# RMS norm and a matmul on one core: another opening, and a last pair of tiles in column blocks

## The chip, the cores and the metric

The kernel runs on one core of a Trainium2 chip. A core has a matrix engine (TensorE, PE in the profile, its weight loads PEld), VectorE (DVE), ScalarE (ACT), GpSimd (POOL) and SyncE (SP, which here only issues transfers), a working memory of 128 partitions (SBUF), accumulator banks that PE writes (PSUM), and 16 DMA engines between SBUF and the device's memory. The metric is the device time of one launch in microseconds (us); less is better.

## The reference

```python
batch, seq, dim, out_dim = 16, 1024, 512, 768
rms = np.sqrt(np.mean(x ** 2, axis=-1, keepdims=True) + eps)
x_norm = x / rms * gamma
return np.matmul(x_norm, weight).astype(np.float32)
```

x has 16,384 rows of 512 floats (33.6 MB), weight is 512 x 768 (1.57 MB), the output 16,384 x 768 floats (50.3 MB). Gamma and eps are inputs.

## The kernel before

The rows are worked on in 128 tiles of 128 rows. Two tiles make a pair j (0 to 63), two pairs a group g (0 to 31) of 512 rows. In a group each partition p holds four rows that lie side by side in memory, so a group's load is 128 pieces of 8 KB (1 MB) and its store 128 pieces of 12 KB (1.5 MB). The row scale 1/rms is applied to the output, gamma to the weights, so the matmuls can start before the norms are known.

For each pair:

- POOL casts x to bf16 (`cast`, L68 to L71).
- ACT squares each tile with a running sum (`squares`, L77), then takes the root (L80); DVE forms the reciprocal (L82).
- PE transposes x. It takes two bf16 values as one 32-bit word, so a tile needs two transposes of 128 x 128 words (`transpose_word`, L92), a pair four. They land in one PSUM tile `tp` (two buffers), and DVE copies the pair to SBUF as `xT` (`evac_words`, L98).
- PE multiplies: four blocks of the inner dimension (k) times two column ranges, 512 and 256 wide, so eight matmuls a tile (L121), into an accumulator of two PSUM banks. There are three accumulators, used in turn.
- ACT scales the first tile of the pair to the output buffer (L130), DVE the second (L132). An output buffer holds a group; there are four, used in turn.
- SP stores the group once its fourth tile is scaled (L136). The last group goes out in two halves.

The order is written out by hand, and each engine and each queue works through its own list in that order; waits are put in for every use of a buffer, among them the wait of a scaling for the store that last read its output buffer. While PE multiplies pair j, the four transposes of pair j + 2 are put between its matmuls (L124, L125), one after every second k. Casts run three pairs ahead, norms one. SP issues the load of group g + 6 at the start of group g (L177), and there are eight input buffers.

The opening (L139 to L173): SP issues the first pair of x (as half a group), the two halves of the weights, the other half of group 0, and groups 1 to 5; group 6 follows at the start of the loop. ACT's queue loads gamma. PE turns gamma to a column (L161). Pair 0 is cast, squared and transposed; DVE scales the four row blocks of the weights to bf16 (`w_bf`, L172). Pair 0 runs its matmuls with k outside and its two tiles inside. Then come the squares of pair 1 and the transposes of pairs 1 and 2, and from pair 1 on the loop is as above.

Of the kernel before, what the change touches and what calls it, by code (L numbers as in the profile page):

```python
# [12 lines left out]
F32 = mybir.dt.float32  # L13
BF16 = mybir.dt.bfloat16
AF = mybir.ActivationFunctionType


@with_exitstack
def kernel(
    ctx: ExitStack,  # L20
    tc: tile.TileContext,
    x: bass.AP,
    gamma: bass.AP,
    weight: bass.AP,
    eps: float,
    out: bass.AP,
):
    nc = tc.nc
    P = 128

    x = x.flatten_outer_dims()
    out = out.flatten_outer_dims()
    N, D = x.shape
    _, O = out.shape
    K = D // P
    G = 4
    NG = N // (P * G)
    NP = 2 * NG
    PF = 6
    SPLITS = [(0, 512), (512, O)]  # L40


    xg = x.rearrange("(g p t) d -> g p t d", p=P, t=G)
    og = out.rearrange("(g p t) o -> g p t o", p=P, t=G)

    singles = ctx.enter_context(tc.tile_pool(name="singles", bufs=1))
    xin = ctx.enter_context(tc.tile_pool(name="xin", bufs=PF + 2))
    xbp = ctx.enter_context(tc.tile_pool(name="xb", bufs=4))
    junk = ctx.enter_context(tc.tile_pool(name="junk", bufs=2))
    stats = ctx.enter_context(tc.tile_pool(name="stats", bufs=4))  # L50
    xt_pool = ctx.enter_context(tc.tile_pool(name="xt", bufs=4))
    tpsum = ctx.enter_context(tc.tile_pool(name="tpsum", bufs=2, space=bass.MemoryType.PSUM))
    opsum = ctx.enter_context(tc.tile_pool(name="opsum", bufs=3, space=bass.MemoryType.PSUM))
    outp = ctx.enter_context(tc.tile_pool(name="out", bufs=4))

    x_tiles, xb_tiles, tp_tiles, rstd_tiles, xT_tiles, o_tiles = {}, {}, {}, {}, {}, {}

    def load(g, parts=1):
        xt = xin.tile([P, G, D], F32, name="xt")
        x_tiles[g] = xt  # L60
        n = G // parts
        for i in range(parts):
            nc.sync.dma_start(out=xt[:, i * n:(i + 1) * n, :], in_=xg[g, :, i * n:(i + 1) * n, :])

    def xpair(j):
        return x_tiles[j // 2][:, 2 * (j % 2):2 * (j % 2) + 2, :]

    def cast(j):  # L68
        xb = xbp.tile([P, 2, D], BF16, name="xb")
        xb_tiles[j] = xb  # L70
        nc.gpsimd.tensor_copy(out=xb, in_=xpair(j))  # L71

    def squares(j):
        ssq = stats.tile([P, 2], F32, name="ssq")
        for t in range(2):
            jk = junk.tile([P, D], BF16, name="jk")
            nc.scalar.activation(out=jk, in_=xpair(j)[:, t, :], func=AF.Square,  # L77
                                 accum_out=ssq[:, t:t + 1])
        rms = stats.tile([P, 2], F32, name="rms")
        nc.scalar.activation(out=rms, in_=ssq, func=AF.Sqrt, scale=1.0 / D, bias=eps_sb)  # L80
        rstd = stats.tile([P, 2], F32, name="rstd")
        nc.vector.reciprocal(out=rstd, in_=rms)  # L82
        rstd_tiles[j] = rstd

    def transpose_word(j, t, h):
        if j not in tp_tiles:
            tp_tiles[j] = tpsum.tile([P, 2, 2, P], F32, name="tp")
        words = xb_tiles[j].rearrange("p a d -> p (a d)").bitcast(F32)  # L90
        lo = t * (D // 2) + h * P
        nc.tensor.transpose(out=tp_tiles[j][:, t, h, :], in_=words[:, lo:lo + P], identity=ident_f)  # L92

    def evac_words(j):
        xb_tiles.pop(j)
        tp = tp_tiles.pop(j)
        xT = xt_pool.tile([P, 2, 2, P, 2], BF16, name="xT")
        nc.vector.tensor_copy(out=xT.rearrange("p t h m c -> p (t h m c)"),  # L98
                              in_=tp.rearrange("p t h m -> p (t h m)").bitcast(BF16))
        xT_tiles[j] = xT  # L100

    def transposes(j):
        for t in range(2):
            for h in range(2):
                transpose_word(j, t, h)
        evac_words(j)

    def matmuls(j, tj=None):
        g, h = j // 2, j % 2
        if h == 0:  # L110
            o_tiles[g] = outp.tile([P, G, O], F32, name="ot")
        ot = o_tiles[g]
        xT = xT_tiles.pop(j)
        rstd = rstd_tiles.pop(j)
        acc = [opsum.tile([P, 2, 512], F32, name="ops").rearrange("p a b -> p (a b)") for _ in range(2)]

        order = [(t, k) for k in range(K) for t in range(2)] if j == 0 else \
                [(t, k) for t in range(2) for k in range(K)]
        for n, (t, k) in enumerate(order):
            for i, (lo, hi) in enumerate(SPLITS):  # L120
                nc.tensor.matmul(out=acc[t][:, lo:hi], lhsT=xT[:, t, k // 2, :, k % 2], rhs=w_bf[:, k, lo:hi],  # L121
                                 start=(k == 0), stop=(k == K - 1))

                if tj is not None and i == 0 and n % 2 == 0:  # L124
                    transpose_word(tj, n // 4, n // 2 % 2)  # L125
            if k < K - 1:
                continue
            dst = ot[:, 2 * h + t, :]
            if t == 0:
                nc.scalar.mul(out=dst, in_=acc[t][:, :O], mul=rstd[:, t:t + 1])  # L130
            else:
                nc.vector.tensor_single_scalar(out=dst, in_=acc[t][:, :O], scalar=rstd[:, t:t + 1],  # L132
                                               op=mybir.AluOpType.mult)

    def store(g, lo=0, hi=G):
        nc.sync.dma_start(out=og[g, :, lo:hi, :], in_=o_tiles[g][:, lo:hi, :])  # L136

    with tc.manual_schedule():
        nc.scalar.preload_act_table(AF.Sqrt)  # L139
        g_row = singles.tile([2, P, 2], F32)  # L140
        nc.scalar.dma_start(out=g_row, in_=gamma.rearrange("(h w c) -> h w c", w=P, c=2))
        w_f32 = singles.tile([P, K, O], F32)

        x0 = xin.tile([P, G, D], F32, name="xt")
        x_tiles[0] = x0
        nc.sync.dma_start(out=x0[:, 0:2, :], in_=xg[0, :, 0:2, :])
        for h in range(2):
            nc.sync.dma_start(out=w_f32[:, 2 * h:2 * h + 2, :],
                              in_=weight[2 * h * P:2 * (h + 1) * P, :].rearrange("(w c) o -> w c o", c=2))
        nc.sync.dma_start(out=x0[:, 2:4, :], in_=xg[0, :, 2:4, :])  # L150
        for g in range(1, PF):
            load(g)

        ident_f = singles.tile([P, P], F32)
        make_identity(nc, ident_f)
        eps_sb = singles.tile([P, 1], F32)
        nc.vector.memset(eps_sb, float(eps))  # L157

        gp = tpsum.tile([P, 2, 2], F32, name="tp")
        for c in range(2):  # L160
            nc.tensor.transpose(out=gp[:, c, :], in_=g_row[:, :, c], identity=ident_f[:2, :2])  # L161
        g_sb = singles.tile([P, 2, 2], F32)
        nc.vector.tensor_copy(out=g_sb, in_=gp)  # L163

        cast(0)
        cast(1)
        squares(0)
        transposes(0)

        w_bf = singles.tile([P, K, O], BF16)  # L170
        for k in range(K):
            nc.vector.tensor_single_scalar(out=w_bf[:, k, :], in_=w_f32[:, k, :], scalar=g_sb[:, k % 2, k // 2:k // 2 + 1],  # L172
                                           op=mybir.AluOpType.mult)  # L173

        for j in range(NP):
            if j % 2 == 0 and j // 2 + PF < NG:
                load(j // 2 + PF)  # L177
            if j + 3 < NP:
                cast(j + 3)
            if j == 0:  # L180
                cast(2)
                matmuls(0)
                squares(1)
                transposes(1)
                transposes(2)
            else:
                if j + 1 < NP:
                    squares(j + 1)
                if j + 2 < NP:
                    matmuls(j, j + 2)  # L190
                    evac_words(j + 2)
                else:
                    matmuls(j)
            g = j // 2
            if g == NG - 1:
                store(g, 2 * (j % 2), 2 * (j % 2) + 2)
            elif j % 2:
                store(g)


# [33 lines left out]
```

## Time and profile before

| | |
|---|---|
| median of 5 runs | 215.09 us (214.63 to 215.16) |
| the profiled execution | 214.63 us, span 212.8 us |
| PE busy | 196.4 us (92%) |
| ACT, DVE, POOL busy | 156.1, 110.6, 67.2 us |
| DMA | 85.69 MB, mean 403 GB/s |
| matmuls (L121), 512 and 256 wide | 382 and 274 ns each as recorded |
| transpose (L92) | 275 ns as recorded |
| evacuation (L98), a pair | 680 ns |
| scaling of a tile on ACT (L130), on DVE (L132) | 901, 1018 ns |
| squares of a tile (L77), root (L80) | 619, 295 ns |
| cast of a pair on POOL (L71) | 1041 ns |
| store of a group, issue to landing | median 10.8 us |
| load of a group, issue to landing | median 12.8 us |

The span runs from the first to the last instruction of the profiled execution; the launch adds some 1.8 us around it. Matmuls are pipelined and the recorded length of one holds its way through the array, so a pace is read from the distance of two starts, not from the length. A chain of waits follows the work that ended last back from the end. For a DMA issue, the time to landing is that until its data is in place, with all that stood before it in the queue.

### The profile page before, as it was taken

The page shows a single profiled execution, that of the slowest core. Times are in us where ns is not written, and L with a number is a line of the kernel's source. Part 1 is how long each engine was busy: PE and PEld are TensorE (multiplying, and loading weights), DVE is VectorE, ACT ScalarE, POOL GpSimd, SP SyncE. Part 2 cuts the span into 40 slices and gives each one's busy share as a digit, 9 for nine tenths or more (in the row PEclk, how much of TensorE's full clock was granted, in tenths as well). Part 3 has the DMA queues.
Part 4 walks back from the last instruction along what each step waited for, and adds up shares of the span by engine and source line. Part 5 has one row for each costly group of instructions (what it writes and reads, how often), then busy time and mean ns, then how long its engine had stood idle before and what let it go on. Part 6 is the DMA issues. An engine that isn't in the chain of part 4 may idle for free.

```text
span 212.8 us, 3556 instructions
## 1 busy us (share of the span) xinstructions
PE 196.4 (92%) x1257; PEld 136.9 (64%) x1282; DVE 110.6 (52%) x198; ACT 156.1 (73%) x385; POOL 67.2 (32%) x70
## 2 busy tenths in 40 slices
PE   0579999999999999999999999999999999999980
PEld 0336777767777777777677777767777777777650
DVE  0525446644664466445644565456545654565451
ACT  2356877787778777877787778777877787778840
POOL 1267323332333223322332233323332333230000
PEclk9999999999999999999999999999999999999997
DMA  5999999999999999999999999999999999967777
GB/s 182 423 425 423 428 423 420 420 426 420 436 429 421 423 423 433 422 426 431 423 429 423 433 415 429 432 432 423 420 426 426 423 435 429 404 270 303 303 297 294
DMA packets 9814, 85.69 MB, mean 403 GB/s; under 512 B 1090, under 2 KB 1092, under 8 KB 1860
## 3 DMA queue, kind: packets, MB, share of 16 engines
q1 hardware_dynamic: 9792, 85.46, 95.7%
q8 instruction: 10, 0.16, 0.3%
q14 instruction: 8, 0.07, 0.1%
q10 hardware_dynamic: 4, 0.00, 0.0%
HBM read 35.13 MB, written 50.33 MB: 402 GB/s over the span
## 4 chain that ended last, share of the span: by engine, by line
PE 91%; DMA 2%; DVE 1%; ACT 1%; issue 1%; POOL 0%
PE ops L121 78%; PE tp L92 13%; DMA xt<-in_x_dram 2%; ACT jk L77 1%; POOL xb L71 0%; DVE ot L132 0%; ACT ot L130 0%; DVE xT L98 0%; DVE w_bf L172 0%; ACT rms L80 0%; DVE rstd L82 0%
## 5 line engine op out<-in xcount | busy, mean ns | idle before, releaser
L121 PE MATMUL ops<-w_bf,xT 128*128 128x256 bf16 (+1 forms) x999 | 193.7, 327 | 3.2 <-DVE w_bf L172 1.3
L121 PEld LDWEIGHTS <-xT 128*128 128x128 bf16 x1024 | 100.7, 98 | 59.2 <-issue 2.1
L132 DVE TENSOR_SCALAR ot<-ops,rstd 128x768 f32<-128x768 f32 x64 | 65.1, 1018 | 88.9 <-PE ops L121 88.9
L71 POOL CAST xb<-xt 128x1024 bf16<-128x1024 f32 x64 | 66.5, 1041 | 122.7 <-PE tp L92 111.8
L130 ACT ACTIVATE ot<-ops,rstd 128x768 f32<-128x768 f32 x64 | 57.7, 901 | 44.5 <-PE ops L121 44.5
L77 ACT ACTIVATE jk<-xt 128x512 bf16<-128x512 f32 x128 | 78.8, 619 | 3.3 <-DMA xt<-in_x_dram 3.3
L92 PE MATMUL tp<-ident_f,xb 128*128 128x128 f32 x256 | 68.9, 275 | 5.2 <-POOL xb L71 5.2
L98 DVE COPY xT<-tp 128x1024 bf16<-128x1024 bf16 x64 | 43.4, 680 | 0.4 <-PE tp L92 0.4
L92 PEld LDWEIGHTS tp<-ident_f,xb 128*128 128x128 f32 x256 | 36.0, 142 | 8.4 <-POOL xb L71 5.5
L77 ACT ACTIVATION_READ_ACCUMULATOR jk<-xt 128x1 f32 x128 | 24.3, 190 | 0.0
L80 ACT ACTIVATE rms<-ssq,eps_sb 128x2 f32<-128x2 f32 x64 | 18.9, 295 | 2.1
L82 DVE RECIPROCAL rstd<-rms 128x2 f32<-128x2 f32 x64 | 9.9, 155 | 5.6 <-ACT rms L80 5.6
L161 PE MATMUL tp<-ident_f,g_row 2*128 2x2 f32 x2 | 0.4, 249 | 2.2 <-DMA g_row<-in_gamma_dram 2.2
L172 DVE TENSOR_SCALAR w_bf<-w_f,g_sb 128x768 bf16<-128x768 f32 x4 | 2.2, 614 | 0.0
L139 ACT ACT_TABLE_LOAD x1 | 1.3, 1283 | 0.7 <-PEq L215 0.7
L161 PEld LDWEIGHTS tp<-ident_f,g_row 2*128 2x128 f32 x2 | 0.3, 200 | 2.2 <-POOL ident_f masks.py:199 2.2
L163 DVE COPY g_sb<-tp 128x4 f32<-128x4 f32 x1 | 0.2, 160 | 1.7 <-PE tp L161 1.7
L157 DVE MEMSET eps_sb<- 128x1 f32 x1 | 0.1, 59 | 0.8 <-PEq L215 0.8
masks.py:199 POOL TENSOR_SCALAR_AFFINE_SELECT ident_f<-ident_f 128x128 f32<-128x128 f32 x1 | 0.3, 293 | 0.1
masks.py:197 POOL MEMSET ident_f<- 128x128 f32 x1 | 0.2, 204 | 0.3 <-POOLq L215 0.3
L215 POOL MEMSET const-float32-0.0<- 128x1 f32 x1 | 0.1, 99 | 0.2 <-issue 0.2
L215 POOL MEMSET const-bfloat16-1.0<- 128x1 bf16 x1 | 0.1, 102 | 0.0
(2 smaller groups left out, 0.2 us busy)
## 6 DMA issues: line engine op xcount, KB each, us to landing
out_dram<-ot SPq DMA_DIRECT2D x31, 1536.0 KB, 10.8
xt<-in_x_dram SPq DMA_DIRECT2D x31, 1024.0 KB, 12.8
w_f<-in_weight_dram SPq DMA_DIRECT2D x2, 768.0 KB, 6.8
out_dram<-ot SPq DMA_DIRECT2D x2, 768.0 KB, 4.0
xt<-in_x_dram SPq DMA_DIRECT2D x2, 512.0 KB, 6.5
g_row<-in_gamma_dram ACTq DMA_DIRECT2D x1, 2.0 KB
```

The source lines that it names most:

```text
L71: nc.gpsimd.tensor_copy(out=xb, in_=xpair(j))
L77: nc.scalar.activation(out=jk, in_=xpair(j)[:, t, :], func=AF.Square, accum_out=ssq[:, t:t + 1])
L80: nc.scalar.activation(out=rms, in_=ssq, func=AF.Sqrt, scale=1.0 / D, bias=eps_sb)
L82: nc.vector.reciprocal(out=rstd, in_=rms)
L92: nc.tensor.transpose(out=tp_tiles[j][:, t, h, :], in_=words[:, lo:lo + P], identity=ident_f)
L98: nc.vector.tensor_copy(out=xT.rearrange("p t h m c -> p (t h m c)"), in_=tp.rearrange("p t h m -> p (t h m)").bitcast(BF16))
L121: nc.tensor.matmul(out=acc[t][:, lo:hi], lhsT=xT[:, t, k // 2, :, k % 2], rhs=w_bf[:, k, lo:hi], start=(k == 0), stop=(k == K - 1))
L130: nc.scalar.mul(out=dst, in_=acc[t][:, :O], mul=rstd[:, t:t + 1])
L132: nc.vector.tensor_single_scalar(out=dst, in_=acc[t][:, :O], scalar=rstd[:, t:t + 1], op=mybir.AluOpType.mult)
L139: nc.scalar.preload_act_table(AF.Sqrt)
L161: nc.tensor.transpose(out=gp[:, c, :], in_=g_row[:, :, c], identity=ident_f[:2, :2])
L172: nc.vector.tensor_single_scalar(out=w_bf[:, k, :], in_=w_f32[:, k, :], scalar=g_sb[:, k % 2, k // 2:k // 2 + 1], op=mybir.AluOpType.mult)
```

## The change

The tiles are cut into segments instead of groups: of 1, 2, 1, 2 and 2 tiles, then 29 of four tiles, then 2, 1 and 1. A segment is what one load, one output buffer and one store hold. Each segment's rows lie side by side in memory: a partition's piece of x is 2 KB for a segment of one tile, 4 KB for two, 8 KB for four. There are ten input buffers in place of eight, still four output buffers and three accumulators.

The opening is written anew. SP issues tile 0, tiles 1 and 2, the weights, and then six more segments of x (tile 3 to tile 23). PE runs twelve matmuls on a zeroed tile, whose result nobody reads, in four batches of three: ahead of the turning of gamma, behind it, behind the transposes of tile 0, and behind those of tiles 1 and 2. Tiles 0 to 2 are cast, transposed and evacuated one by one, tiles 0 and 1 cast by DVE. The weights' row blocks are scaled by DVE (0 and 2) and by ACT (1 and 3). Tiles 0, 1 and 2 run their matmuls for k = 0 and 1 first, side by side in three accumulators, then for k = 2 and 3 one by one, each followed by its scaling. Tile 3 follows, with the transposes of pair 2 between its last matmuls.

In the loop, which begins with pair 2, pairs 2 to 5 carry the transposes of the next pair, pair 6 those of pairs 7 and 8, and the later ones those of the pair after next as before. The evacuation is now put into DVE's list right behind the pair's fourth transpose, ahead of the odd tile's scaling. One segment is loaded whenever a pair begins a new segment.

For the last two tiles the matmuls run the 512 columns first for all k, then the 256, into an accumulator of their own each. ACT scales the wide block and stores it on its own queue, DVE scales the narrow one and SP stores it.

```diff
-    PF = 6
+    XBUFS = 10
+    sizes = [1, 2, 1, 2, 2] + [G] * (NT // G - 3) + [2, 1, 1]
+    first = [sum(sizes[:s]) for s in range(NS)]
+    def rows(ap, s):
+        return ap[first[s] * P:(first[s] + sizes[s]) * P, :].rearrange("(p t) d -> p t d", t=sizes[s])
...
+    def evac(j, t=0, n=2):
+        if j not in xT_tiles:
+            xT_tiles[j] = xt_pool.tile([P, 2, 2, P, 2], BF16, name="xT")
+        src = tp_tiles.pop(j).rearrange("p t h m -> p t (h m)").bitcast(BF16)
+        dst = xT_tiles[j].rearrange("p t h m c -> p t (h m c)")
+        nc.vector.tensor_copy(out=dst[:, t:t + n, :], in_=src[:, t:t + n, :])
...
+    def out_tile(i):
+        s = seg_of[i]
+        if s not in o_tiles:
+            o_tiles[s] = outp.tile([P, G, O], F32, name="ot")
+        return o_tiles[s][:, i - first[s], :]
+    def store(i):
+        s = seg_of[i]
+        if i == first[s] + sizes[s] - 1:
+            nc.sync.dma_start(out=rows(out, s), in_=o_tiles[s][:, :sizes[s], :])
...
+        load(0)
+        load(1)
...
+        for s in range(2, XBUFS - 1):
+            load(s)
...
+        def warm_up(n):
+            for _ in range(n):
+                nc.tensor.matmul(out=spare[:, :WIDE], lhsT=warm[:, :P], rhs=warm, start=True, stop=True)
...
+        warm_up(3)
...
+        warm_up(3)
+        ssq = stats.tile([P, 4], F32, name="ssq")
+        cast(0, nc.vector)
+        square(0, ssq[:, 0:1])
+        transpose_tile(0)
+        warm_up(3)
+        cast(1, nc.vector)
+        cast(2, nc.gpsimd)
+        square(1, ssq[:, 1:2])
+        square(2, ssq[:, 2:3])
+        transpose_tile(1)
+        transpose_tile(2)
+        warm_up(3)
+        acc = [accumulator() for _ in range(4)]
+        weights(0, nc.vector)
+        weights(1, nc.scalar)
+        for k in (0, 1):
+            for i in range(3):
+                matmuls(i, acc[i], [k])
+        root(0, 3, ssq)
+        weights(2, nc.vector)
+        weights(3, nc.scalar)
+        cast(3, nc.gpsimd)
+        matmuls(0, acc[0], [2, 3])
+        finish_tile(0, acc[0], nc.scalar)
+        transpose_tile(3)
+        norms(3, 1)
+        matmuls(1, acc[1], [2, 3])
+        finish_tile(1, acc[1], nc.vector)
+        cast(4, nc.gpsimd, 2)
+        matmuls(2, acc[2], [2, 3])
+        finish_tile(2, acc[2], nc.scalar)
+        matmuls(3, acc[3], [0, 1, 2, 3], feeder([2], [0, 0, 2, 2]))
+        finish_tile(3, acc[3], nc.vector)
+        cast(6, nc.gpsimd, 2)
+        cast(8, nc.gpsimd, 2)
+        norms(4, 2)
+        one, two, both = [0, 0, 1, 0, 1, 1, 1, 0], [1, 0, 1, 0, 1, 0, 1, 0], [1, 1, 1, 1, 1, 1, 1, 1]
+        loaded = XBUFS - 1
+        for j in range(2, NP):
+            if seg_of[2 * j] > seg_of[2 * j - 1] and loaded < NS and loaded < seg_of[2 * j] + XBUFS - 1:
+                load(loaded)
+                loaded += 1
...
+            if j < 6:
+                feed = feeder([j + 1], one)
+            elif j == 6:
+                feed = feeder([7, 8], both)
+            elif j + 2 < NP:
+                feed = feeder([j + 2], two)
+            for i, engine in ((2 * j, nc.scalar), (2 * j + 1, nc.vector)):
+                a = accumulator()
+                matmuls(i, a, range(K), feed)
+                finish_tile(i, a, engine)
+        for i in (NT - 2, NT - 1):
+            s = seg_of[i]
+            for lo, hi, engine, queue in ((0, WIDE, nc.scalar, nc.scalar), (WIDE, O, nc.vector, nc.sync)):
+                a = accumulator()
+                for k in range(K):
+                    matmul(i, k, a, lo, hi)
+                dst = out_tile(i)[:, lo:hi]
+                scale(engine, dst, a[:, lo:hi], rstd_of[i])
+                queue.dma_start(out=rows(out, s)[:, 0, lo:hi], in_=dst)
```

`feeder(pairs, gaps)` gives a function that `matmuls` calls between the 512- and the 256-wide matmul of each k; each call issues as many transposes of the listed pairs as the list says, and the evacuation behind a pair's fourth.

## The prediction

> **What bounds the kernel now.** I read the page first (busy shares, slices), then the chain of waits, then the order of time at both ends, then the DMA issues with their times to landing.
>
> ```profile
> PE 196.4 (92%) x1257; PEld 136.9 (64%) x1282; DVE 110.6 (52%) x198; ACT 156.1 (73%) x385; POOL 67.2 (32%) x70
> ...
> PE   0579999999999999999999999999999999999980
> ...
> DMA  5999999999999999999999999999999999967777
> ```
>
> PE is full from slice 3 to the last but one, and the DMA engines are full too until the loads end near 187 us. PE is the bound: ACT's scalings of the even tiles start at 194.29, 197.32 and 200.36, so a pair takes 3.034 us, and without transposes (203.18, 205.78) 2.60 us. A tile's eight matmuls are thus 1.30 us and one transpose is (3.034 - 2.60)/4 = 0.108 us. The work is 128 x 1.30 + 256 x 0.108 = 194.1 us; PE ends at 207.0, so about 13 us are lost before its even pace, which begins with pair 1 at 16.43 (chain of waits, start, length, what):
>
> ```profile
> 0.74 4.57 DMA xt<-in_x_dram
> 5.37 1.04 POOL xb L71
> 6.46 1.13 PE tp L92 x4
> 8.88 4.23 PE ops L121 x14
> 13.14 0.90 ACT ot L130
> 14.04 1.23 ACT jk L77 x4
> 16.43 0.39 PE ops L121
> ```
>
> Pair 0 costs 4.6 us, not 2.6, and then PE waits for an evacuation that stands on DVE behind a reciprocal, behind ACT's squares and scaling. Pair 7, whose transposes and those of pair 8 are the first state that both kernels share, starts at 16.43 + 6 x 3.034 = 34.63. The forecast is when the new kernel reaches that point.
>
> Why pair 0 is slow shows in the weight loads in order of time:
>
> ```profile
> 9.91 0.36 PEld L121 LDWEIGHTS <-xT 128*128 128x128 bf16 x2 [0.28 <-issue]
> 10.55 0.36 PEld L121 LDWEIGHTS <-xT 128*128 128x128 bf16 x2 [0.28 <-issue]
> ```
>
> 512 + 256 columns take 0.64 us here, 0.325 later: half rate until about 12.5, 3.6 us after the first matmul. The granted clock reads 1.00 all the while, so it doesn't show this.
>
> **The opening, part by part.** *Loads.* x for tile 0 alone (0.26 MB), tiles 1 and 2 (0.52), the weights (1.57), then 1, 2, 2 and four times 4 tiles: 24 tiles queued at once as before. Before, 0.52, 1.31 and 2.10 MB into the stream landed at 5.3, 7.3 and 9.1. By the same rates (254 GB/s at first, 406 to 425 later) tile 0 lands at 4.4, tiles 1 and 2 at 6.0, the weight halves at 7.9 and 9.75 (0.65 later, for the tile put ahead of them), tile 3 at 10.5, pair 2 at 11.6. SP issues one in 0.4 us and is ahead of the data.
>
> *Up to the matmuls.* The cast of tile 0 moves to DVE: between 0.34 us (half an evacuation, 680 ns) and 0.61 (the 768-column scaling of the weights, 614 ns); I take 0.45. Twelve idle matmuls go into PE's waits for x and w, each at most 0.427 us (half rate); the last three end at 7.7 to 8.9. One weight row block goes to ACT (about 0.9, as a scaling). The first matmul starts at 8.65, as before (8.88).
>
> *Three tiles on half the weights.* k = 0, 1 for tiles 0 to 2 are 6 x 0.325 = 1.95 us, to 10.6, when w_bf 2 and 3 are just ready. The rest of the three tiles (1.95), tile 3's transposes (0.22), tile 3 and the transposes of pair 2 (1.73) end at 14.45. Pair 2's evacuation can only start 0.16 after its last transpose (as 199.62 to 199.78 shows), takes 0.68 and PE follows 0.05 later: a stall of 0.67. Pair 2 starts at 15.1; before, at 19.46.
>
> *One pair ahead, not two.* In pairs 2 to 5 the last of the next pair's transposes stands 0.43 us of matmuls before the pair's end, and the evacuation needs 0.89 less the 0.108 of that transpose: 0.35 us of stall in each, 1.4 together. Pair 6 carries eight transposes, 3.47. Pair 7 then starts at 15.1 + 4 x 3.39 + 3.47 = 32.1: 2.5 us early. If the idle matmuls don't bring the full rate by 8.65, the half-rate stretch moves with the matmuls: 1.9 + 0.25 late, 34.3, still 0.3 early.
>
> The page "TensorE: Matmul & The Clock Gate" of the Trainium skill (Part 1, Part 4) says that about 3.4 us of sustained matmuls lift the rate and that transposes don't count as busy in the same way. The 3.6 us above agree; the idle matmuls here are cut by transposes and waits, so the rule leans to the later figure.
>
> *What takes its place: the output buffers.* There are four, one per segment now. Tile 0, pair (1, 2), tile 3 and pair 2 take them, so the scaling of tile 6 (the fifth segment) must wait until tile 0's store has landed. That store is issued near 12.1, behind all 24 tiles in SP's queue. How stores fare there, the first store of before shows (its issue with us to landing; the first 22.5 us as one window, last figure GB/s; the instruction queue's packets, MB and share of 16 engines in 26 to 27 us):
>
> ```profile
> out_dram<-ot SPq DMA_DIRECT2D x1, 1536.0 KB, 9.5
> ...
> 0.00:22.50 22.50, 13.13 (x69) 8.29 (x71) 7.41 (x16) 10.56 (x25) 9.04 (x15) 1.00 0.92 367
> ...
> q8 instruction: 1, 0.02, 6.8%
> ```
>
> Issued at 20.78, it landed at 30.3, though its 1.57 MB are 3.7 us of transfer: it went behind loads not yet moved. Its stream position, 8.91 + 1.57 = 10.49 MB, had been moved at 27.8 (mean 378 GB/s); the last load ahead of it (issued 7.29, landed 18.1 later, at 25.4) did so 1.3 after its bytes had moved (8.91 MB, 24.1), and in 26 to 27 one instruction fetch held a single DMA engine for 6.8% of 16 us, 1.09: 27.8 + 1.3 + 1.09 = 30.2. For tile 0's store: 6.29 + 1.57 + 0.39 = 8.26 MB, moved at 22.5 (367 GB/s x 22.5), so it lands at 23.8, or 24.9 with such a fetch. The fetch came after some 100 matmuls; the new kernel reaches that number near 22, so I take L = 24.9. Short packets at the start can only delay it: x's first packets, of 4 KB, moved at about 56 per us (28 in 2.0 to 2.5). Whether that is a limit of bytes or of packets is open; if of packets, tile 0's 2 KB ones cost up to 1.0 us more. L is from 23.8 to 25.9.
>
> From L: tile 6 scaled by L + 0.95. Tile 9 takes tile 6's accumulator (three in turn), so it starts at L + 1.0; PE would have been there at 23.3. ACT's squares for pair 5 are behind tile 6's scaling (2 x 0.61 + root, to L + 2.5), DVE's reciprocal behind them, and pair 5's evacuation behind that, L + 2.7 to 3.4. So pair 5 starts at L + 3.45, pair 6 at L + 6.84, pair 7 at L + 10.3. With L = 24.9 that is 35.2 against 34.63: **0.6 us later**. The point of no change is L = 24.3. The clock's question drops out, as both PE paths (32.1, 34.3) are earlier.
>
> *Even pace.* The same instructions on PE, ACT, DVE and POOL; evacuations move ahead of the odd tile's scaling on DVE (idle 88.9 us before these), worth nothing. The loads lead by 28 tiles as before. Stores landed after at most 14.1 us and a buffer is wanted again after 19.7.
>
> **The tail.** Tiles 126 and 127 get four stores of column blocks, rows of 2 KB on ACT's queue and 1 KB on SP's. PE's time is the same; the last scaling shrinks from 1.02 to about 0.4. But look what the DMA engines do (windows; the last two figures are their share and GB/s):
>
> ```profile
> 204.00:205.00 1.00, 1.00 (x9) 0.61 (x7) 0.52 (x1) 0.08 (x1) 0.00 (x0) 1.00 0.92 393
> ...
> 208.00:209.00 1.00, 0.00 (x0) 0.00 (x0) 0.10 (x1) 0.00 (x0) 0.00 (x0) 1.00 1.05 424
> ...
> 210.00:211.00 1.00, 0.00 (x0) 0.00 (x0) 0.00 (x0) 0.00 (x0) 0.00 (x0) 0.75 1.00 406
> ```
>
> From 204 to 211.2 they are full: the four-tile store issued at 203.0 and the two after it are 3.15 MB, and at about 410 GB/s they end 4.1 us after PE. The new tail moves the same 3.15 MB after the same four-tile store, so an earlier issue gains nothing; at best 0.3 of landing. Short packets may cost: nothing if bytes decide (the 4 KB packets of x's second half ran at about 100 per us after 8 us, full rate), and 512 packets at the opening's 56 per us would be 9 us for 1.9. Between these the 4 KB row is nearer, as a queue stood behind it too; I take 0.2.
>
> The page "DMA: Bandwidth & Descriptors" (Specifications) puts the line rate at packets of 512 B and up. By it the tail's term is 0 and the sum 0.6.
>
> **Sum.** 0.6 + 0.2 = +0.8 us on the profiled execution, 214.63 (span 212.8 and 1.8 around it). That run is the fastest of five; on their median, 215.09, it gives 215.9, and I say 215.8.
>
> **Rivals.** *The opening's gain survives (faster).* Tile 0's store lands by 23.8, no fetch falls on it and the packets are cheap: pair 7 at 34.1, -0.5; if the store slips ahead of the loads, the PE paths hold, -0.3 to -2.5. It decides below L = 24.1. For it: PE's own path is shorter on either clock. Against it: the 9.5 us. 214.4, down to 212.6.
>
> *They cancel*, L of 24.1 to 24.6 or a tail at nothing: 215.1.
>
> *The short rows rule the tail.* Rows of 1 and 2 KB at half rate end it 1.9 later: 217.5 with the opening's term.
>
> **How the numbers follow.** A measurement can tell about 0.2%, 0.43 us. Slot wait decides: 0.47. Gain survives: 0.26. Cancel: 0.20. Short rows: 0.07. Faster 0.26, same 0.22 (part of the first case is under 0.43), slower 0.52. The forecast's own range is 215.2 to 216.9 (L to 25.9, tail to 0.5); with one gain in three left out below and most of the short rows above, 214.0 to 217.0.
>
> **What would show it.** In the profile after: ACT's and DVE's scaling of tiles 6 and 7 waiting for the store's DMA until 24 to 26, PE idle before tile 9 and pair 5; 0.35 us gaps before pairs 3 to 6; DMA full to the end. I am wrong if PE is without a gap from 15 us on, or if the DMA engines fall idle before the last stores.

## The result, and the profile after

The changed kernel takes 216.97 us (median of 27 runs, 214.90 to 218.62) against 215.08 us before (48 runs, 214.23 to 216.86). The ratio is 1.0064, with a 95% interval of 1.0043 to 1.0086: slower by some 1.4 us. The ratio compares runs of one chip with each other and leaves disturbed ones out, so it isn't the ratio of the two medians. The profiled execution of the changed kernel took 215.59 us, span 213.8, against 214.63 and 212.8.

The page shows the same two full engines (busy shares, PE and DMA in 40 slices):

```profile
PE 201.0 (94%) x1269; PEld 137.7 (64%) x1294; DVE 111.8 (52%) x202; ACT 158.1 (74%) x388; POOL 66.6 (31%) x71
...
PE   7598989999999999999999999999999999999980
...
DMA  6999999999999999999999999999999999967777
```

PE is busy 4.6 us longer; the idle matmuls alone are 5.1. The difference in time lies at both ends. In the opening, the order of time shows PE's waits (start, length, what, idle before and releaser; these are the starts of pairs 2, 3, 4, 5 and 6):

```profile
17.59 1.04 PE L137 MATMUL ops<-w_bf,xT 128*128 128x512 bf16 x5 [0.67 <-ACT jk L78]
...
21.16 1.04 PE L137 MATMUL ops<-w_bf,xT 128*128 128x512 bf16 x5 [0.35 <-DVE xT L108]
...
24.72 1.04 PE L137 MATMUL ops<-w_bf,xT 128*128 128x512 bf16 x4 [0.35 <-DVE xT L108]
...
28.28 1.04 PE L137 MATMUL ops<-w_bf,xT 128*128 128x512 bf16 x5 [0.35 <-DVE xT L108]
...
31.84 0.39 PE L137 MATMUL ops<-w_bf,xT 128*128 128x512 bf16 x1 [0.35 <-DVE xT L108]
```

Pairs 2 to 5 take 3.56 us, not 3.03. Pair 6 carries eight transposes (3.47), so pair 7 starts at 35.3; before, it started at 34.63. The opening lost 0.7 us.

The store of tile 0 and the scaling of tile 6 that needs its buffer (DMA issue with us to landing, issued at 14.63; then ACT's order of time):

```profile
out_dram<-ot SPq DMA_DIRECT2D x1, 384.0 KB, 10.0
```

```profile
21.47 0.30 ACT L82 ACTIVATE rms<-ssq,eps_sb 128x2 f32<-128x2 f32 x1
24.76 0.90 ACT L118 ACTIVATE ot<-ops,rstd 128x768 f32<-128x768 f32 x1 [3.00 <-DVE xT L108]
```

The store landed at 24.63 and ACT stood idle for 3.00 us until then. The releaser is named as an evacuation, since that signalled last by the profile's count; the runs below name the DMA. In this execution PE was late by itself, and here is why (windows; PE's busy time comes first, the granted clock is the figure before the last two):

```profile
8.00:9.00 1.00, 0.00 (x0) 0.00 (x0) 0.28 (x1) 0.30 (x1) 0.00 (x0) 1.00 0.98 399
9.00:10.00 1.00, 0.61 (x3) 0.27 (x3) 0.49 (x2) 0.82 (x2) 0.00 (x0) 0.54 1.04 420
10.00:11.00 1.00, 1.00 (x4) 0.44 (x3) 0.54 (x2) 0.51 (x1) 0.00 (x0) 0.50 1.03 422
...
12.00:13.00 1.00, 1.00 (x6) 0.50 (x5) 0.00 (x0) 0.00 (x0) 0.53 (x1) 0.75 1.01 426
```

The last idle matmuls ended at 7.45, the weights came at 8.7, and PE was without work for 1.9 us. The 0.54 and the 0.75 put the ends of the half clock at 9.1 and 12.5, one window of 3.4 us that begins shortly before the matmuls do. The sixteen matmuls that start at 9.39 took 4.27 us.

The other 0.3 us lie behind PE's end: from the start of the last scaling to the end of the span it is 212.8 - 207.08 = 5.7 us before and 213.8 - 207.75 = 6.05 after. The DMA engines are full there as before.

### The profile page after: what moved, and what is told of

It is laid out like the page before. It is cut to its first block, busy times and chain, and to the rows that moved or that the text cites. A ratio compares the mean times of both kernels' runs of the same rounds, so it can differ in the third digit from the quotient of the medians.

```text
span 213.8 us, 3607 instructions
## 1 busy us (share of the span) xinstructions
PE 201.0 (94%) x1269; PEld 137.7 (64%) x1294; DVE 111.8 (52%) x202; ACT 158.1 (74%) x388; POOL 66.6 (31%) x71
## 4 chain that ended last, share of the span: by engine, by line
PE 89%; DMA 3%; DVE 2%; ACT 2%; issue 1%; SPq 0%; DVEq 0%
PE ops L137 76%; PE tp L101 13%; DMA w_f<-in_weight_dram 3%; DVE xT L108 1%; ACT jk L78 1%; ACT ot L118 1%; SPq L65 0%; DVE w_bf L120 0%; DVE ot L120 0%; ACT rms L82 0%; DVEq L120 0%
## 5 line engine op out<-in xcount | busy, mean ns | idle before, releaser
L137 PE MATMUL ops<-w_bf,xT 128*128 128x512 bf16 (+1 forms) x999 | 194.5, 326 | 5.2 <-DVE w_bf L120 1.9
L74 POOL CAST xb<-xt 128x1024 bf16<-128x1024 f32 (+1 forms) x65 | 65.9, 1014 | 124.4 <-PE tp L101 107.4
L118 ACT ACTIVATE ot<-ops,rstd 128x768 f32<-128x768 f32 (+1 forms) x65 | 58.0, 893 | 41.8 <-PE ops L137 38.0
L108 DVE COPY xT<-tp 128x1024 bf16<-128x1024 bf16 (+1 forms) x66 | 44.5, 675 | 84.4 <-PE tp L101 84.3
L120 DVE TENSOR_SCALAR ot<-ops,rstd 128x768 f32<-128x768 f32 (+1 forms) x65 | 64.5, 992 | 2.6 <-PE ops L137 2.4
L82 ACT ACTIVATE rms<-ssq,eps_sb 128x2 f32<-128x2 f32 (+1 forms) x64 | 18.9, 296 | 2.0
L84 DVE RECIPROCAL rstd<-rms 128x2 f32<-128x2 f32 (+1 forms) x64 | 9.9, 155 | 4.5 <-ACT rms L82 4.5
L189 PE MATMUL ops<-warm 128*128 128x512 bf16 x12 | 5.1, 555 | 1.2 <-DVE eps_sb L182 1.2
L118 ACT ACTIVATE w_bf<-w_f,g_sb 128x768 bf16<-128x768 f32 x2 | 1.9, 935 | 2.9 <-DMA w_f<-in_weight_dram 2.9
L189 PEld LDWEIGHTS <-warm 128*128 128x128 bf16 x12 | 1.3, 124 | 2.2 <-DVE eps_sb L182 1.2
```

The source lines that it names most:

```text
L74: engine.tensor_copy(out=xb_tiles[i // 2][:, i % 2:i % 2 + n, :], in_=xtile(i, n))
L82: nc.scalar.activation(out=rms[:, :n], in_=ssq[:, :n], func=AF.Sqrt, scale=1.0 / D, bias=eps_sb)
L84: nc.vector.reciprocal(out=rstd[:, :n], in_=rms[:, :n])
L108: nc.vector.tensor_copy(out=dst[:, t:t + n, :], in_=src[:, t:t + n, :])
L118: nc.scalar.mul(out=dst, in_=src, mul=r)
L120: nc.vector.tensor_single_scalar(out=dst, in_=src, scalar=r, op=mybir.AluOpType.mult)
```

## The experiments

Two theories stood against each other. S is the forecast's: tile 0's store, behind 24 tiles of loads in SP's queue, holds its output buffer, and that sets when the even pace begins. P says that PE's own list (half rate, late evacuations) decides and ACT's wait lies beside it, as the profiled execution above suggests. All ratios below are to the kernel before.

### Six output buffers

```diff
-    outp = ctx.enter_context(tc.tile_pool(name="out", bufs=4))
+    outp = ctx.enter_context(tc.tile_pool(name="out", bufs=6))
```

> The changed kernel with six output buffers in place of four; nothing else. No scaling can then wait for tile 0's store. Theory S (the forecast's: the wait for that store decides when the even pace begins): pair 7 starts earlier than in the changed kernel by 0.4 to 1 us and the ratio to before falls from 1.0064 to about 1.003. Theory P (PE's own list decides: half rate in the opening and the late evacuations of pairs 2 to 6, with ACT's 3.0 us wait for the store lying beside it): ACT's wait before tile 6 is gone, pair 7 still starts near 35.3 us, ratio 1.0064 within 0.1%.

Measured: 213.52 us, ratio 0.9924 (0.9891 to 0.9956). One number takes 1.4% off and makes the changed kernel 0.8% faster than the one before. ACT's order of time has tile 6's scaling wait for PE alone:

```profile
21.29 0.90 ACT L118 ACTIVATE ot<-ops,rstd 128x768 f32<-128x768 f32 x1 [1.01 <-PE ops L137]
```

The store itself still landed at 24.6 (issued at 13.13, 11.5 us). S holds, and the gain of some 3 us is larger than the 0.4 to 1 that I gave it; P's "no change" falls. In the profiled execution pair 6 starts at 30.36, which is 1.5 us earlier than in the first profile of the changed kernel and 2.0 earlier than in the second, below; the rest of the 3 us isn't followed in a trace.

### Earlier transposes

```diff
-        matmuls(3, acc[3], [0, 1, 2, 3], feeder([2], [0, 0, 2, 2]))
+        matmuls(3, acc[3], [0, 1, 2, 3], feeder([2], [2, 2, 0, 0]))
-        one, two, both = [0, 0, 1, 0, 1, 1, 1, 0], ...
+        one, two, both = [1, 0, 1, 1, 1, 0, 0, 0], ...
```

> The changed kernel with the transposes of the next pair put earlier into pairs 2 to 5 (the fourth two k earlier) and those of pair 2 at the first two k of tile 3. Theory P: the four stalls of 0.53 us and some 0.6 of the 0.94 before pair 2 go, pair 7 starts near 32.6, 2.7 us earlier, ratio about 0.994. Theory S: tile 6's scaling still waits until 24.7, tile 9 and pair 5's evacuation follow it, pair 7 starts near 34.7, 0.6 earlier, ratio about 1.003.

Measured: 216.61 us, ratio 1.0033 (0.9991 to 1.0074): S's figure; P's 0.994 lies outside the interval. PE's stalls were gone, pair 2 started at 15.0, and PE then ran into the wait. In order of time, ACT's scaling of tile 6 and PE's start of tile 9:

```profile
25.10 0.90 ACT L118 ACTIVATE ot<-ops,rstd 128x768 f32<-128x768 f32 x1 [5.66 <-DMA out_dram<-ot]
...
26.05 0.59 PE L137 MATMUL ops<-w_bf,xT 128*128 128x512 bf16 x1 [3.18 <-ACT ot L118]
```

A window behind that wait shows a new cost, the granted clock at 0.50 (from 25.8 to 29.2):

```profile
27.00:28.00 1.00, 1.00 (x5) 0.38 (x4) 0.42 (x2) 0.97 (x4) 1.00 (x1) 0.50 1.03 430
```

### Twelve idle matmuls in the last batch

```diff
         transpose_tile(2)
-        warm_up(3)
+        warm_up(12)
```

> The changed kernel with twelve idle matmuls in place of three in the last batch, so that PE isn't idle from 7.45 to 9.39 us while it waits for the weights. Theory P: the granted clock stays at 1.00 past 9 us, the first sixteen real matmuls take 2.6 us instead of 4.27, pair 7 starts 1.4 to 1.7 us earlier, ratio about 0.999. Theory S: the clock is better all the same, but the store of tile 0 still lands near 24.7, pair 7 starts at 34.9 or later, 0.4 us earlier at most, ratio about 1.004 to 1.006. If idle matmuls do nothing to the rate, both: no change.

Measured: 215.72 us, ratio 1.0032 (1.0001 to 1.0062). The clock stayed at 1.00. P's 0.999 lies just outside the interval and S's 1.004 to 1.006 in it, and the trace decides for S. The chain that the forecast wrote down stands in this trace step by step. ACT's scaling of tile 6 started at 24.61, released by the DMA, and PE's order of time goes on:

```profile
25.56 0.38 PE L137 MATMUL ops<-w_bf,xT 128*128 128x512 bf16 x1 [1.13 <-ACT ot L118]
27.90 1.04 PE L137 MATMUL ops<-w_bf,xT 128*128 128x512 bf16 x5 [0.55 <-DVE xT L108]
31.46 0.39 PE L137 MATMUL ops<-w_bf,xT 128*128 128x512 bf16 x1 [0.35 <-DVE xT L108]
```

Tile 9, pair 5 and pair 6 start 0.95, 3.29 and 6.85 after 24.61; the forecast had 1.0, 3.45 and 6.84 after L.

### All three

> All three edits together: six output buffers, earlier transposes in pairs 2 to 5, twelve idle matmuls in the last batch. Both theories: neither the store nor PE's stalls are left, pair 7 starts 4 us earlier than in the changed kernel, near 31.2, ratio about 0.988 if the whole of it reaches the end. If the DMA engines bound the end instead (they are full until 187 us and again in the last 8), less than half of it reaches the end, ratio about 0.998.

Measured: 212.67 us, ratio 0.9897 (0.9863 to 0.9931). Each of the last two edits by itself moved the ratio by 0.3%, and on top of the buffers the two add 0.3% together; neither step is clear of the intervals. The last scaling started at 203.95 and not at 206.26 (with six buffers alone), 2.3 us earlier, but the spans are 211.2 and 212.3: half of that is given back at the end.

### Fewer loads ahead of the store

```diff
-        for s in range(2, XBUFS - 1):
+        for s in range(2, 7):
             load(s)
-        loaded = XBUFS - 1
+        loaded = 7
```

> The changed kernel with four output buffers as it has them, but with seven segments of x issued at the start in place of nine (16 tiles ahead of tile 0's store in SP's queue, not 24); the other two come in the loop. Theory S (the store waits behind the loads that are queued ahead of it): 2.1 MB less at about 425 GB/s let tile 0's store land 4.9 us earlier, near 19.8, ACT's wait before tile 6 is gone, and the ratio falls to that of six buffers, about 0.992. Theory B (it is the number of buffers, or another use of them, and not the place in the queue): the ratio stays at 1.006. Against both: if the shorter lead starves the casts later, POOL waits for x and PE for POOL, and it is slower than 1.006.

The changed kernel issues nine segments ahead of the loop: two before the weights and seven (not six) behind them, segments 2 to 8, of which two are held back here.

Measured: 215.25 us, ratio 1.0017 (0.9984 to 1.0050): neither theory's figure. No scaling waited for a store, and pair 6 started at 29.28. In the profiled execution, one of the longest (217.07 us), the gain was lost later, by what the last sentence of the expectation had feared. From the waits (total us, times, longest), and a window of the profile near the end:

```profile
POOL xb L74 <- DMA xt<-in_x_dram: 131.9, 35, 5.3
```

```profile
200.00:202.00 2.00, 0.00 (x0) 0.00 (x0) 0.00 (x0) 1.42 (x4) 0.20 (x1) 1.00 0.43 178
```

POOL waited for x over the whole kernel (in the changed kernel 12.5 us in 7 waits), and at 200 us PE stood idle for 2.6 us, until a late load had come (201.8) and been cast. This run alone settles nothing about the queue.

### Fewer loads ahead of the store, caught up in the loop

```diff
-            if seg_of[2 * j] > seg_of[2 * j - 1] and loaded < NS and loaded < seg_of[2 * j] + XBUFS - 1:
-                load(loaded)
-                loaded += 1
+            for _ in range(2):
+                if seg_of[2 * j] > seg_of[2 * j - 1] and loaded < NS and loaded <= seg_of[2 * j] + 6 - (j == 2) * 2 - (j == 3):
+                    load(loaded)
+                    loaded += 1
```

> The changed kernel with four output buffers and seven segments of x issued at the start, as in the run with fewer loads, but the loop catches up with the missing two over pairs 2 to 4, so that from pair 4 on the loads lead as in the changed kernel. Theory S: tile 0's store lands near 20, no scaling waits for it, no cast starves later, and the ratio is that of six buffers, 0.992 (0.990 to 0.996). Theory B (the number of buffers counts, not the place in the queue): 1.006. If it stays near 1.002 as with fewer loads, the shorter lead was not what held that kernel back.

Measured: 213.06 us, ratio 0.9931 (0.9905 to 0.9957), with four buffers as in the changed kernel. Tile 0's store was issued at 12.69 and landed 8.4 us later, at 21.1 (not quite the 19.8 to 20 hoped for; the DMA engines moved only 266 GB/s in 14 to 16 us). Tile 6's scaling:

```profile
21.22 0.90 ACT L118 ACTIVATE ot<-ops,rstd 128x768 f32<-128x768 f32 x1 [1.38 <-DMA out_dram<-ot]
```

It waited 1.38 us, too short to reach PE. So it is the place in the queue, and the buffers are one way around it. Theory B falls.

### The changed kernel, another execution

> The changed kernel as it is, for a second look beside the others of this call. Ratio 1.006. Theory S adds: where the first matmuls run at full rate, PE comes to tile 9 before the store has landed, stands idle for 1 to 3 us, and an idle of 2 us or more costs the granted clock for one window of 3.4 us behind it (0.50), another 1.7 us; where the first matmuls run at half rate, PE comes late by itself and the wait is hidden.

Measured: 216.12 us, ratio 1.0069 (1.0045 to 1.0094). In this execution the clock was at 1.00 throughout the opening, and it gained nothing by it. Pair 2 started at 14.52, 3 us earlier than in the first profile, and then (ACT's order of time, then PE's):

```profile
25.49 0.90 ACT L118 ACTIVATE ot<-ops,rstd 128x768 f32<-128x768 f32 x1 [6.79 <-DMA out_dram<-ot]
```

```profile
26.44 0.38 PE L137 MATMUL ops<-w_bf,xT 128*128 128x512 bf16 x1 [3.21 <-ACT ot L118]
28.77 1.04 PE L137 MATMUL ops<-w_bf,xT 128*128 128x512 bf16 x5 [0.55 <-DVE xT L108]
32.34 0.39 PE L137 MATMUL ops<-w_bf,xT 128*128 128x512 bf16 x1 [0.35 <-DVE xT L108]
```

Pair 7 follows at 32.34 + 3.47 = 35.8, 1.2 us later than before. Whether PE comes early or late, it is stopped near the same time. An idle of 3.21 us cost no clock here, so the second half of the expectation held only in part. This execution also shows the whole of the change's cost without any loss of clock: pair 7 is 1.2 us late, the end behind the last scaling 0.3 longer (6.06 against 5.7), and the spans differ by 214.3 - 212.8 = 1.5.

### Ordinary last tiles

```diff
-        for i in (NT - 2, NT - 1):
-            s = seg_of[i]
-            for lo, hi, engine, queue in (...):
...
+        for i, engine in ((NT - 2, nc.scalar), (NT - 1, nc.vector)):
+            a = accumulator()
+            matmuls(i, a, range(K))
+            finish_tile(i, a, engine)
```

> The changed kernel with the last two tiles as ordinary tiles (scaled whole, stored by SP with rows of 3 KB); the opening as changed. Theory R (short rows cost 0.35 us): ratio 1.005 against 1.0064. Theory N: equal. If the column blocks earn their latency: 1.009 or more.

Measured: 217.04 us, ratio 1.0115 (1.0088 to 1.0141), which looks as if the column blocks helped by 0.5%. The trace doesn't bear that out: from the start of the last scaling to the end it is 215.7 - 209.72 = 5.98 us, against 214.3 - 208.24 = 6.06 with column blocks in the other execution of the changed kernel. What differs is the opening, whose code is the same. PE waited 2.58 us before tile 9, began at 26.90, and 0.6 us later got half its clock (PE's order of time, then windows):

```profile
26.90 0.38 PE L137 MATMUL ops<-w_bf,xT 128*128 128x512 bf16 x1 [2.58 <-ACT ot L118]
```

```profile
27.00:28.00 1.00, 1.00 (x6) 0.68 (x6) 0.00 (x0) 1.00 (x4) 0.00 (x0) 0.75 1.07 449
28.00:29.00 1.00, 1.00 (x6) 0.66 (x4) 0.26 (x2) 0.97 (x3) 0.00 (x0) 0.50 0.99 415
```

Pair 6 started 7.87 us after tile 6's scaling, not 6.85. The mean granted clock was 0.976 to 0.984 in four of this kernel's six runs and in none of the changed kernel's six beside it; the two runs without the loss took 216.17 and 216.26 us. The kernel before, which has no such wait, also has runs like these: on the chip of the first experiments ten of 34, at 216.6 to 216.8 us and 0.984 or 0.985. So the loss isn't tied to this wait alone. Between these two executions the tail's edit is a matter of 0.1 us, and the ratio doesn't measure it.

The same edit was made where nothing stops PE in the opening, on the kernel with all three edits:

> The kernel with all three edits (six buffers, earlier transposes, twelve idle matmuls), but with the last two tiles as ordinary tiles, each scaled whole and stored by SP with rows of 3 KB. Theory R (rows of 1 and 2 KB slow the end): 0.3 to 0.4 us faster than with column blocks, ratio 0.988 against 0.9897. Theory N (the end is bound by the bytes behind the last four-tile store): equal within 0.1 us. If the column blocks help, 0.5 us slower or more, ratio 0.992.

Measured: 212.71 us, ratio 0.9883 (0.9837 to 0.9929), against 0.9897 with column blocks: the same.

### No idle matmuls

All three edits, with every `warm_up` call taken out.

> All three edits, but with no idle matmul at all. If the idle matmuls raise the rate in time: the first 3.4 us of real matmuls run at half rate, 1.4 to 1.8 us slower than with them, ratio 0.997. If the rate would be raised by the transposes anyway, or the loss is hidden: equal, 0.990.

Measured: 212.99 us, ratio 0.9889 (0.9846 to 0.9932), the same as with them. The first sixteen matmuls took 4.75 us instead of 2.76, so the idle matmuls do raise the rate (the first line is without them, the second with):

```profile
8.15 4.75 PE L137 MATMUL ops<-w_bf,xT 128*128 128x512 bf16 x16 [1.26 <-DVE w_bf L120]
```

```profile
9.48 2.76 PE L137 MATMUL ops<-w_bf,xT 128*128 128x512 bf16 x16 [0.29 <-DVE w_bf L120]
```

Those without them also started 1.3 us earlier, as the weights had come earlier in that execution, so the last scaling started only 0.7 us later (204.62 against 203.95). The span is 211.0 against 211.2: even that isn't seen at the end.

### The last segments stored by pairs

```diff
+        t = i - first[s]
+        if s >= NS - 6 and sizes[s] == G:
+            if t % 2:
+                nc.sync.dma_start(out=rows(out, s)[:, t - 1:t + 1, :], in_=o_tiles[s][:, t - 1:t + 1, :])
+        elif t == sizes[s] - 1:
-        if i == first[s] + sizes[s] - 1:
```

On the kernel with all three edits:

> All three edits, and the last three segments of four tiles stored as two pairs each in place of one store; column blocks as in the changed kernel. The DMA engines are idle for 2 us or so before the last four-tile store and then full to the end. Theory N (bytes that come late bound the end): the first half of those bytes goes out 2.6 us earlier, the end comes 1 to 1.9 us earlier, ratio 0.982 to 0.985 against 0.9897. If the end hangs on the latency of the last store alone: no change.

Measured: 212.81 us, ratio 0.9883 (0.9842 to 0.9925). No gain. With ordinary last tiles as well:

> Six buffers, earlier transposes, twelve idle matmuls, the last three four-tile segments stored by pairs, the last two tiles as ordinary tiles. If the DMA engines' backlog bounds the end, as the equal times of the four kernels before suggest: ratio 0.986 to 0.989. If each of the two tail edits earns 0.3 to 1 us: 0.983.

Measured: 212.40 us, ratio 0.9899 (0.9885 to 0.9913), the fastest median, and within what the others show. Its windows behind PE's end (203.4) show what is still moved there:

```profile
206.00:207.00 1.00, 0.00 (x0) 0.00 (x0) 0.00 (x0) 0.00 (x0) 0.00 (x0) 1.00 0.62 249
207.00:208.00 1.00, 0.00 (x0) 0.00 (x0) 0.00 (x0) 0.00 (x0) 0.00 (x0) 0.61 0.05 22
208.00:209.00 1.00, 0.00 (x0) 0.00 (x0) 0.00 (x0) 0.00 (x0) 0.00 (x0) 0.50 0.07 28
```

The bytes did go out earlier, and by the mean share most engines were done by 207. But for 2.3 us more, to 209.3, the share is 0.05 to 0.07, and one engine of sixteen is 0.0625: about one engine's worth of work is left over. My reading that the mean backlog bounds the end is not enough for these kernels. That it is one engine is read from the mean share, and why it would fall behind was not settled.

## Why the prediction was right, and where it was not

The forecast was 215.8 us and "slower" as the likeliest, by the wait for tile 0's store; the ratio on 215.08 gives 216.5, inside the range.

*The output buffers.* This step held. L was taken as 24.9; four executions with four buffers and three idle matmuls in the last batch gave 24.6, 25.0, 25.4 and 25.9 (landing of the store), one with twelve 24.6. The chain from there to pair 6 was right to 0.1 us, in part by luck: pair 5 came 0.16 sooner behind L than I gave, and the pair after it took 3.56 where I gave 3.39. Two independent edits that take the wait away, more buffers and fewer loads ahead, give the same ratio, 0.992 and 0.993. Of the parts of L, the first was right: the 8.26 MB had been moved at 22.6 to 23.1 us in these executions and the one with six buffers (mean rate from the start times the time), against 22.5, so short packets at the start cost at most 0.6 where up to 1.0 was feared. The landing came 1.6 to 2.8 later, against 1.3 + 1.09. The 1.09 for an instruction fetch isn't shown: the fetch fell between 19 and 25 us, and its time doesn't sort the landings (in 23 to 24 us L was 24.6 with six buffers and 25.9 with ordinary last tiles). That L came out in the middle of what was measured is thus partly luck. The two latest values come with stretches of slow transfer (254 and 315 GB/s in 20 to 21 and 21 to 22 us where L was 25.4), but so does an early one (279 and 341 with twelve idle matmuls, 24.6); the cause is open.

*"The clock's question drops out".* This was wrong, in two ways. PE's idle time, which the wait makes, can go with a loss of clock: two of the executions above lost one window of 3.4 us at 0.50 with it, about 1 us in the one where the chain can be followed, and one didn't. And in the first profile, the half rate and the stalls made PE late enough by themselves (35.3) to hide the wait, so that its chain of waits doesn't name the store at all, and PE was not idle before tile 9, though that was forecast. That these 35.3 are nearly the 35.2 of the forecast is luck: there they came by another road. The page "TensorE: Matmul & The Clock Gate" of the Trainium skill (Part 1) has both the window of 3.4 us and the fall of the rate after idle time. I weighed it only for the warming up and not for the wait that I predicted; it speaks of an idle window of about 3.4 us, while here 1.9 us were enough once and 3.21 were not another time, and once the clock fell 0.6 us after PE had begun to work again. What decides it was not found.

*The stall per pair.* I gave 0.35 us and it was 0.53 (3.56 less 3.03). The rows before pairs 3 to 6 do show an idle of 0.35, but that is counted from the recorded end of a matmul and not a loss of pace, so its agreement with my number is chance. The step that failed is the 0.16 from the last transpose to its evacuation. In the row that I read, DVE had been kept by a scaling, and that evacuation wasn't released by the transpose before it (DVE's order of time in the profile before):

```profile
198.84 1.02 DVE L132 TENSOR_SCALAR ot<-ops,rstd 128x768 f32<-128x768 f32 x1 [1.35 <-PE ops L121]
199.78 0.68 DVE L98 COPY xT<-tp 128x1024 bf16<-128x1024 bf16 x1
```

Where DVE is free it is 0.31 (the profile after, PE's and DVE's order of time):

```profile
20.10 0.27 PE L101 MATMUL tp<-ident_f,xb 128*128 128x128 f32 x1
```

```profile
20.41 0.69 DVE L108 COPY xT<-tp 128x1024 bf16<-128x1024 bf16 x1 [0.78 <-PE tp L101]
```

Over four pairs the 0.53 in place of 0.35 is 0.7 us.

*The weights* came at 8.7 and 10.5, not 7.9 and 9.75, and the first real matmul at 9.39 instead of 8.65; in the second execution of the same kernel it came at 7.83. In the first profile this and the stalls, less what the half rate fell short of its 2.15 us (it cost 1.5, 4.27 against 2.76), made PE's path 1.0 us longer than the 34.3 that I gave. It hardly mattered, since the store decided in the other four executions with four buffers and 24 tiles ahead.

*The tail.* "The same bytes behind the same store" held: nothing was gained by earlier issue. Its term of 0.2 was 0.3 on the profiled executions, of which the column blocks as a whole make 0.1 (6.06 against 5.98, one execution each). What the short rows cost and what the shorter last scaling saves (0.48 against 1.02) aren't told apart, so the rows may cost up to 0.6. The rival in which short rows rule the tail by 1.9 falls. The page "DMA: Bandwidth & Descriptors" of the Trainium skill (Specifications) puts the line rate at transfers of 512 B and up; by it these rows cost nothing, which the runs neither contradict nor show.

*The sum.* 0.8 us was forecast and about 1.4 measured. In the second execution the terms can be set side by side: 1.2 where 0.6 was given, mainly by L (25.4 where 24.9 was taken, 25.9 in the latest), and 0.3 for the tail where 0.2 was given. The clock lost in other executions had no term. It isn't needed for the 1.4: five of the six runs beside that second execution had a mean clock of 0.995 to 0.998, and the ratio was 1.0069 all the same.

## What to carry to other kernels

Where loads and stores share a queue, a deep prefetch delays the first stores by the bytes that stand ahead of them (here tile 0's store landed at 24.6 to 25.9 us behind 24 tiles of loads and at 21.1 behind 16); if the buffers are cut into small segments, the wait for the first store comes round after as many tiles as the segments hold. Write down for each buffer when it is wanted again, in bytes of queue ahead of its release, before making the work in front of it faster. And look at two or three executions before believing one chain of waits: here one of them hid the wait that decided the others.

## What the runs showed of the hardware

- Near idle time of PE the granted clock can fall, and not always: 1.9, 3.18 and 2.58 us of idle came with one window of 3.4 us at 0.50 each, while 3.21 us in the changed kernel did not. The window began 0.3 and 0.2 us before PE's next matmul in the first two, and 0.6 us after it in the third.
- The granted clock reads 1.00 while the first matmuls run at half rate in the kernel before and in the one without idle matmuls (4.75 us for sixteen), yet 0.50 in the changed kernel after its first rise. There three idle matmuls took 1.35 us at 4.59 and 0.81 at 6.64, with the clock at 1.00 in both. In these traces the figure can't be trusted before the first rise; the distance of two starts can.
- At the end of the fastest kernel about one DMA engine's worth of transfer goes on for 2.3 us after the rest is done, and the span ends only behind it (at 210.6).
